# First pass of the input projection: two chunk counts and the number of warming products

## The chip, the cores and the metric

The kernel runs on one core of one Trainium2 chip. The metric is the device time of one execution in microseconds (us); the time before is the median of three runs. Beside the runs stands one execution taken with the hardware profiler, from which all views of the profile come.

## The reference

Two layers of an encoder over 256 tokens of width 2048 (batch 1, float32). Each layer makes six modulation vectors from a conditioning vector `c`, then a mixer sub-layer and a gated feed-forward sub-layer. What matters here is the beginning of the first layer:

```python
c_act = jax.nn.silu(c)
mod = c_act @ ada_w[l] + ada_b[l]
sh_a, sc_a, gt_a, sh_m, sc_m, gt_m = [t[:, None, :] for t in jnp.split(mod, 6, axis=-1)]

h = rmsnorm(x, norm_mix[l]) * (1.0 + sc_a) + sh_a
qa, ka, va, qb, kb, vb, ga, gb = split_cols(h @ w_in[l])
```

`h @ w_in` has 2048 input channels and 8704 output columns: 4608 for the queries, keys and values of two attention branches, then 2048 for each of two gates. After it come the two attentions, two projections, the gates, one output projection, and the feed-forward part.

## The kernel before

**Weights.** All big weights lie in one stream of 128x128 blocks, in the order in which TensorE uses them (`block_stream`, line 108). Sixteen blocks (1 MB) are one load. `unit_steps` (line 345) brings a load by a DMA on SyncE's queue into one of four buffers (`rawp`, line 172) and splits it into a high half (ScalarE cast, line 362) and a low half (VectorE subtraction, line 363), in two parts of eight blocks. Four buffers hold split halves (`hlp`, line 173). Every product is made of three: high x high, high x low, low x high (lines 480 to 482).

**The chunks of h.** x lies on the chip with the 2048 channels in 16 chunks of 128. One chunk of h needs two entries of the modulation: the scale and the shift of its 128 channels. Each such entry is a vector product with a 1 MB transfer (`ada`, line 243: the transfer on line 259, the product on VectorE on line 262; after a scale, line 271 makes `amod`). Then `normed` (line 570) makes the chunk: `ht` on VectorE (line 576), its high half on ScalarE (line 587), its low half on VectorE (line 588). So a chunk is three steps: two products and the chunk itself (`ada_and_h`, line 829).

**The start.** Squares of x are summed, two small matmuls (line 876) give the mean square, ScalarE adds epsilon (line 879), GpSimd takes the root (line 567), TensorE spreads it over the partitions by two transposes (line 558), ScalarE copies that to `rbs` (line 562), which each `ht` reads. Between these steps TensorE runs products that nothing reads (`warm`, line 515): `WARM_IN` (line 69) gives their number before the sums of squares, between these and the spread, and after the spread. `WARM_ROW` more follow the very first piece of work on weights (line 484).

**The passes.** In the first layer the projection for queries, keys and values goes over nine groups of 512 columns (four blocks), and over the first gate. As the chunks of h come one by one, this is done in three passes (`K_ENDS`, line 41): in the first pass group g takes chunks 0 up to its first number, and the gate's columns take chunks 0 to 5; the second pass goes on from there; the third takes the rest. `tokens` (line 468) runs one group of one pass: for each of its chunks, four blocks of the stream and six matmuls of 128x512, three for each half of the 256 tokens. At a group's end the sums are copied from PSUM by ScalarE in the first pass (line 1042, for the gate line 1078), and added by VectorE in the later ones (line 1044).

**What sets the order.** `next_block` (line 433) calls for load u + 1 when it begins load u, so one load is called ahead. At the end of each load `tick` (line 426) runs steps of `ada_and_h` until their number is on the line `FIRST_PLAN` (line 64), a table of (load, steps): 6 steps at load 0, 17 at load 10, 48 at load 42. Before a group begins, `have_h` (line 1025) runs further steps if one of its chunks has not been called yet; such steps are not counted for the line. The calls make a program in order, from which the compiler's scheduler places the instructions on each engine, with its own idea of what will be ready; each engine then runs its queue in the order so fixed, but for places that the code pins.

The table, and the pinned product that changes its number:

```python
K_ENDS = [
    [([2, 2, 2, 3, 3, 4, 4, 4, 4], 6), ([7, 7, 9, 9, 9, 10, 10, 11, 12], 13), ([KC] * 9, KC)],
...
FIRST_PLAN = [(0, 6), (10, 17), (42, 48)]
...
        warm(WARM_IN[1])
        nc.scalar.activation(out=mean_sq[:], in_=ps[:], func=AF.Identity, bias=eps[:])
```

## Time and profile before

| | us |
|---|---|
| median of three runs | 2586.0 |
| lowest and highest run | 2583.72, 2588.13 |
| profiled execution | 2584.38 |
| its span, first to last instruction | 2582.6 |
| TensorE (PE) busy | 2545.2 |
| VectorE (DVE) busy | 2209.7 |
| ScalarE (ACT) busy | 1451.2 |
| GpSimd (POOL) busy | 255.2 |

Times in the views are in us from the span's start, "mean ns" excepted. A line of the timeline gives start, duration, engine, line of the kernel, operation, what is written <- what is read, shapes and count, and in brackets the idle time before it and what ended that. A line of the waits gives who waited for whom, then the total in us, the number of times and the longest. A line of the busy time by stretches gives the stretch, its length, the busy time and number of instructions of PE, PEld (TensorE's weight loads), DVE, ACT and POOL, then the granted TensorE clock as a share of full speed, the mean busy share of the DMA engines and their GB/s. Matmul ends are modelled, so matmuls that run back to back show longer durations than the steps between their starts.

### The profile page before, as it was taken

The numbers are of one execution on the slowest core, as the hardware profiler recorded it, in microseconds if no ns is written. First come the engines' busy times: TensorE is split into PE (matmuls) and PEld (weight loads), VectorE is DVE, ScalarE is ACT, GpSimd is POOL, SyncE is SP. The second block draws the span as 40 slices with busy tenths as digits, with TensorE's granted clock in tenths as the row PEclk, the third lists the DMA queues.
The fourth block names the chain that finished last, engine by engine and source line by source line (L and its number), as shares of the span: only waits on it lengthen the run. The fifth ranks groups of instructions, "written<-read, shape, count | busy, mean of one in ns | idle before, by whom it ended". The sixth has DMA issues, their size and how long they took to land.

```text
span 2582.6 us, 41196 instructions
## 1 busy us (share of the span) xinstructions
PE 2545.2 (99%) x16204; PEld 2341.1 (91%) x16204; DVE 2209.7 (86%) x3179; ACT 1451.2 (56%) x2400; POOL 255.2 (10%) x345
## 2 busy tenths in 40 slices
PE   8999999999999999999999999999999999999999
PEld 6788888899999999999998889999999999999998
DVE  8899999898998899799987778879889987766775
ACT  5445765446653665466565666644576546654663
POOL 0000100000000000000004668730000000000000
PEclk9999999999999999999999999999999999999999
DMA  9998779886777777777767667778847775555554
GB/s 370 347 348 303 270 306 359 340 304 224 263 294 305 260 282 295 291 278 279 287 221 276 259 228 258 261 290 324 308 177 292 291 295 197 206 201 197 204 203 147
DMA packets 102149, 699.84 MB, mean 271 GB/s; under 512 B 12865, under 2 KB 15169, under 8 KB 18113
## 3 DMA queue, kind: packets, MB, share of 16 engines
q1 hardware_dynamic: 101954, 697.20, 72.8%
q8 instruction: 127, 2.08, 0.3%
q14 instruction: 68, 0.56, 0.1%
HBM read 695.06 MB, written 2.10 MB: 270 GB/s over the span
## 4 chain that ended last, share of the span: by engine, by line
PE 73%; DVE 14%; DMA 4%; issue 3%; ACT 3%; POOL 2%; SPq 0%; DVEq 0%; ACTq 0%; POOLq 0%
PE ps L405 31%; PE ps L406 15%; DVE hl L363 5%; PE ps_t L481 5%; PE ps_t L482 5%; PE ps_t L480 5%; DVE aw L262 4%; PE ps L411 3%; PE ps L409 3%; PE ps L410 3%; DMA aw<-in_aw 3%; ACT hl L362 1%; POOL p L334 1%; POOL packA L334 1%; DMA p<-in_bias 1%
## 5 line engine op out<-in xcount | busy, mean ns | idle before, releaser
L363 DVE TENSOR_TENSOR hl<-w,hl 128x1024 fp32r<-128x1024 f32 x928 | 1130.5, 1226 | 220.3 <-ACT hl L362 217.7
L362 ACT CAST hl<-w 128x1024 fp32r<-128x1024 f32 x928 | 963.3, 1046 | 590.8 <-PE ps L406 258.0
L405 PE MATMUL ps<-h,hl 128*128 128x512 f32 x2432 | 796.8, 382 | 0.0
L406 PE MATMUL ps<-h,hl 128*128 128x256 f32 x2432 | 662.9, 273 | 0.0
L405 PEld LDWEIGHTS ps<-h,hl 128*128 128x128 f32 x2432 | 459.7, 189 | 63.9
L406 PEld LDWEIGHTS ps<-h,hl 128*128 128x128 f32 x2432 | 466.9, 192 | 0.0
L262 DVE CUSTOM_DVE_ANT_0 aw<-aw,cact,ab 128x2048 f32<-128x2048 f32 x189 | 444.3, 2352 | 12.4 <-DMA aw<-in_aw 12.3
L481 PE MATMUL ps_t<-hl,h 128*128 128x512 f32 x832 | 318.5, 383 | 7.4 <-DVE hl L363 7.0
L480 PE MATMUL ps_t<-hl,h 128*128 128x512 f32 x832 | 314.9, 383 | 5.5 <-ACT hl L362 2.9
L482 PE MATMUL ps_t<-hl,h 128*128 128x512 f32 x832 | 315.9, 380 | 0.0
L481 PEld LDWEIGHTS ps_t<-hl,h 128*128 128x128 f32 x832 | 158.1, 190 | 33.8 <-DVE hl L363 12.0
L480 PEld LDWEIGHTS ps_t<-hl,h 128*128 128x128 f32 x832 | 157.3, 190 | 30.0 <-ACT hl L362 4.8
L482 PEld LDWEIGHTS ps_t<-hl,h 128*128 128x128 f32 x832 | 158.1, 190 | 22.1
L405 PE MATMUL ps<-act_o,hl 128*128 128x512 f32 x512 | 170.5, 382 | 0.0
L1189 DVE SCALAR_TENSOR_TENSOR u<-both,cw,u 128x255 f32<-128x255 f32 x304 | 146.3, 481 | 3.8
L411 PE MATMUL ps<-merged,hl 128*128 128x256 f32 x512 | 140.9, 276 | 4.4 <-DVE hl L363 4.4
L409 PE MATMUL ps<-merged,hl 128*128 128x256 f32 x512 | 140.8, 276 | 0.8 <-ACT hl L362 0.4
L410 PE MATMUL ps<-merged,hl 128*128 128x256 f32 x512 | 140.6, 275 | 0.0
L406 PE MATMUL ps<-act_o,hl 128*128 128x256 f32 x512 | 139.6, 273 | 0.0
L1211 ACT COPY both<-ps 128x256 f32<-128x256 f32 x152 | 56.2, 370 | 123.8 <-PE ps L406 122.7
L1162 DVE SCALAR_TENSOR_TENSOR x<-ps,mod,x 128x256 f32<-128x256 f32 x224 | 105.4, 482 | 21.0 <-PE ps L406 18.9
L405 PE MATMUL ps<-act_y,hl 128*128 128x512 f32 x352 | 118.3, 382 | 0.0
(267 smaller groups left out, 4656.6 us busy)
## 6 DMA issues: line engine op xcount, KB each, us to landing
w<-in_ws SPq DMA_DIRECT2D x463, 1024.0 KB, 4.9
aw<-in_aw SPq DMA_DIRECT2D x189, 1024.0 KB, 5.0
p<-in_bias SPq DMA_DIRECT2D x16, 256.0 KB, 4.6
x<-in_xT SPq DMA_DIRECT2D x4, 512.0 KB, 5.6
aw_o<-in_aw SPq DMA_DIRECT2D x2, 1024.0 KB, 12.5
out<-x SPq DMA_DIRECT2D x16, 128.0 KB, 2.4
w<-in_ws SPq DMA_DIRECT2D x2, 512.0 KB, 11.7
aw_b<-in_aw SPq DMA_DIRECT2D x1, 1024.0 KB, 17.9
```

The source lines that it names most:

```text
L262: product = nc.vector.tensor_tensor_reduce(out=raw[:], in0=raw[:], in1=cact[:], scale=1.0, scalar=ab[:, i : i + 1], op0=ALU.mult, op1=ALU. ...
L362: nc.scalar.copy(hl[:, 0], r)
L363: nc.vector.tensor_tensor(out=hl[:, 1], in0=r, in1=hl[:, 0].bitcast(F32), op=ALU.subtract)
L405: nc.tensor.matmul(ps[:], hi, act.both, start=first, stop=False)
L406: nc.tensor.matmul(ps[:, :S], lo, act.high, start=False, stop=last)
L409: nc.tensor.matmul(out, hi, act[0], start=first, stop=False)
L410: nc.tensor.matmul(ps[:, :S], hi, act[1], start=False, stop=False)
L411: nc.tensor.matmul(out, lo, act[0], start=False, stop=last)
L480: nc.tensor.matmul(ps[:], xh, hi, start=kc == kcs[0], stop=False)
L481: nc.tensor.matmul(ps[:], xh, lo, start=False, stop=False)
L482: nc.tensor.matmul(ps[:], xl, hi, start=False, stop=kc == kcs[-1])
L1189: nc.vector.scalar_tensor_tensor(out=u[:, to], in0=ps[:, of], scalar=w[:, j : j + 1], in1=u[:, to], op0=ALU.mult, op1=ALU.add)
```

## The change

In the first pass the fourth group takes two chunks of h instead of three, and the sixth three instead of four; the second pass takes up what they leave, as its own numbers stay. The stream of weights changes its order with it, since it is made from the same table. Of the products between the sums of squares and the spread of the root, four are left of twelve.

```diff
 K_ENDS = [
-    [([2, 2, 2, 3, 3, 4, 4, 4, 4], 6), ([7, 7, 9, 9, 9, 10, 10, 11, 12], 13), ([KC] * 9, KC)],
+    [([2, 2, 2, 2, 3, 3, 4, 4, 4], 6), ([7, 7, 9, 9, 9, 10, 10, 11, 12], 13), ([KC] * 9, KC)],
     [([KC] * 9, KC)],
 ]
...
-WARM_IN = [8, 12, 6]
+WARM_IN = [8, 4, 6]
```

## The prediction

> **What bounds the kernel now.** I read the page first, for the span and the engines, then the waits of TensorE (PE) by stretches, then the busy time by stretches, then the timeline of the first 120 us. The page:

> ```profile
> span 2582.6 us, 41196 instructions
> PE 2545.2 (99%) x16204; PEld 2341.1 (91%) x16204; DVE 2209.7 (86%) x3179; ACT 1451.2 (56%) x2400; POOL 255.2 (10%) x345
> ```

> PE is busy 99% of the span, so there is little to win anywhere. The change concerns the first pass, which lies in the first 120 us. Busy time of PE, PEld, DVE (VectorE), ACT (ScalarE) and POOL in four stretches, then the granted clock, the DMA share and GB/s:

> ```profile
> 24.30:60.00 35.70, 31.75 (x140) 25.60 (x139) 31.99 (x38) 21.34 (x31) 0.00 (x0) 1.00 0.96 376
> 60.00:100.00 40.00, 37.53 (x168) 31.31 (x169) 34.79 (x37) 20.90 (x29) 0.00 (x0) 1.00 0.94 355
> 100.00:120.00 20.00, 18.29 (x85) 15.72 (x84) 16.70 (x27) 8.92 (x10) 0.00 (x0) 1.00 0.88 322
> 120.00:200.00 80.00, 79.91 (x371) 69.66 (x370) 77.81 (x88) 32.91 (x36) 0.00 (x0) 1.00 0.93 351
> ```

> Up to 120 us PE, VectorE and the DMA engines are all near full, and no one of them alone is the bound; from 120 to 200 us PE has no gap. What PE waits for (total us, times, longest), from 26 to 60, 60 to 100 and 100 to 150 us:

> ```profile
> PE ps_t L480 <- ACT h L587: 1.8, 2, 1.1
> PE ps_t L480 <- ACT hl L362: 1.5, 1, 1.5
> PE ps_t L481 <- DVE hl L363: 0.2, 1, 0.2
> ```
> ```profile
> PE ps_t L481 <- DVE hl L363: 1.4, 3, 0.6
> PE ps_t L480 <- ACT hl L362: 1.4, 3, 0.6
> ```
> ```profile
> PE ps_t L481 <- DVE hl L363: 1.7, 1, 1.7
> ```

> The sum is 8.0 us: all that a better order of the first passes can bring. It is small gaps, each where a chunk of h or the halves of a weight load come late.

> **The warming products.** Eight of twelve leave the queue of PE. The timeline of the start:

> ```profile
> 13.69 2.92 PE L520 MATMUL warm<-ident 128*128 128x128 f32 x24
> ...
> 14.20 1.68 POOL L567 TENSOR_TENSOR nrs<-ms_in,mhalf 128x2 f32<-128x2 f32 x1 [12.21 <-ACT ms_in L879]
> ...
> 15.24 2.35 DVE L262 CUSTOM_DVE_ANT_0 aw<-aw,cact,ab 128x2048 f32<-128x2048 f32 x1
> ...
> 16.45 0.38 PE L558 MATMUL rb<-ident,nrs 128*128 128x128 f32 x2
> ...
> 16.86 0.37 ACT L562 COPY rbs<-rb 128x256 f32<-128x256 f32 x1 [2.74 <-PE rb L558]
> ...
> 17.63 0.16 DVE L271 SCALAR_TENSOR_TENSOR amod<-mod,nrm 128x1 f32<-128x1 f32 x1
> 17.90 0.48 DVE L576 SCALAR_TENSOR_TENSOR ht<-x,amod,rbs 128x256 f32<-128x256 f32 x1
> ```

> Twelve products are 24 matmuls in 2.92 us, 0.122 each; four end near 14.7. The root is ready at 14.20 + 1.68 = 15.9, and the spread, at 16.45 now, can start some 0.5 us earlier; rbs then ends near 16.7 instead of 17.2. But ht, the first chunk of h, also needs amod, which stands behind the second vector product (15.24 to 17.6) and itself ends at 17.8. So the 0.5 us ends in a wait that is there anyway: worth 0. The bounds are -0.5 (if VectorE took the chunk ahead of that product, which it can't, since amod needs it) and what a colder clock would cost. The cover for it is the product; with that gone 0.5 us would be gained. The clock is where this edit could do harm. PE would idle from 14.7 to 15.9 and again after the spread's own warming. The nearest rows are a longer gap later on:

> ```profile
> 276.63 0.48 PE L774 MATMUL tp<-ident,p 128*128 128x128 f32 x1 [2.55 <-ACT p L763]
> ```
> ```profile
> 270.00:280.00 10.00, 7.45 (x30) 6.07 (x30) 8.74 (x18) 6.05 (x18) 0.00 (x0) 0.83 0.84 297
> ```

> A gap of 2.55 us is followed by a mean clock of 0.83 over 10 us, which is 0.17 x 10 / 0.5 = 3.4 us at half speed, a loss of at most 1.7 us; the 1.7 us gap of the third wait list left the clock at 1.00 (row 100 to 120). An idle of 1.2 us is nearer to the second. I take 0; even half speed there would be largely hidden, since sixteen warming products (L484) stand between the first piece and the next weights.

> [...]

> **The two moved pieces.** Call one chunk of h through one group of four blocks a piece: six matmuls. 34 steps lie between these two rows:

> ```profile
> 107.73 0.38 PE L481 MATMUL ps_t<-hl,h 128*128 128x512 f32 x1
> ...
> 115.07 0.38 PE L482 MATMUL ps_t<-hl,h 128*128 128x512 f32 x1
> ```

> so one matmul is 7.34 / 34 = 0.216 us, a piece 1.30, a load (16 blocks, 1 MB) four pieces or 5.18. Two pieces leave the first pass and stand in the second: PE work, loads, copies (L1042) and adds (L1044) are the same in number, so this is 0 by itself. What moves is the need and the calls. Counting pieces from 0, chunk 2 of h is needed in piece 10 instead of 8, chunk 3 in 17 instead of 15; chunk 4 in 30 instead of 32 and chunk 5 in 31 instead of 33, because the gates begin two pieces sooner. Of the calls (a: a product of L262 with its transfer; h: a chunk; w: a load) the old order is a4 a5 w2 h2 a6 w3 a7 h3 w4 a8 w5 a9 w6 h4 w7 a10 a11 h5 w8 a12 w9 a13 w10 h6; the new one a4 a5 w2 h2 w3 a6 w4 a7 h3 a8 w5 a9 w6 h4 w7 a10 a11 h5 a12 w8 a13 w9 h6 w10. On SyncE w3 passes a6, w4 passes a7, and from w8 to w15 one more step is ahead; with the ninth chunk of h, which the old code calls out of turn at piece 62, both are level again by load 16.

> Chunks 2 and 3, VectorE, ACT and PE:

> ```profile
> 31.60 2.35 DVE L262 CUSTOM_DVE_ANT_0 aw<-aw,cact,ab 128x2048 f32<-128x2048 f32 x1
> ...
> 34.18 0.48 DVE L576 SCALAR_TENSOR_TENSOR ht<-x,amod,rbs 128x256 f32<-128x256 f32 x1
> ...
> 35.12 1.98 ACT L362 CAST hl<-w 128x1024 fp32r<-128x1024 f32 x2
> ...
> 36.18 2.36 DVE L363 TENSOR_TENSOR hl<-w,hl 128x1024 fp32r<-128x1024 f32 x2 [0.45 <-ACT hl L362]
> 36.20 1.13 PE L480 MATMUL ps_t<-hl,h 128*128 128x512 f32 x4 [1.53 <-ACT hl L362]
> ...
> 38.46 2.35 DVE L262 CUSTOM_DVE_ANT_0 aw<-aw,cact,ab 128x2048 f32<-128x2048 f32 x1
> ```
> ```profile
> 40.73 2.36 DVE L363 TENSOR_TENSOR hl<-w,hl 128x1024 fp32r<-128x1024 f32 x2
> ...
> 46.66 0.48 PE L480 MATMUL ps_t<-hl,h 128*128 128x512 f32 x1 [0.74 <-ACT h L587]
> ```

> At 36.20 PE waits 1.53 us for the cast of w2, not for chunk 2: VectorE and ACT ran chunk 2 first, though w2 was called first. A chunk holds them 36.18 - 34.18 = 2.0 us, a product 40.73 - 38.46 = 2.27. Piece 8 still needs w2, and nothing in the change puts w2 ahead of chunk 2: the gap stays (between -1.5 and 0; 0 by the order of this row). Chunk 3 (0.74) is needed 2.6 us later, but a7 now gets the buffer that w2 frees at 38.5, not the one that a5 frees at 33.95 (31.60 + 2.35), and w3 and w4 stand before it: supply slips by as much as the need. Between -0.74 and +1.5; 0.

> Chunk 5 and w8:

> ```profile
> 70.96 2.36 DVE L363 TENSOR_TENSOR hl<-w,hl 128x1024 fp32r<-128x1024 f32 x2 [0.45 <-ACT hl L362]
> 73.24 2.35 DVE L262 CUSTOM_DVE_ANT_0 aw<-aw,cact,ab 128x2048 f32<-128x2048 f32 x1
> ```
> ```profile
> 70.98 0.70 PE L480 MATMUL ps_t<-hl,h 128*128 128x512 f32 x2 [0.52 <-ACT hl L362]
> 71.93 0.70 PE L480 MATMUL ps_t<-hl,h 128*128 128x512 f32 x2 [0.25 <-ACT hl L362]
> ```

> PE comes to w8 as it is made. VectorE is free at 70.96 - 0.45 = 70.5; with a12 ahead, the low halves start near 70.5 + 2.3 = 72.8 and the first (half of 2.36) is there at 74.0. PE has high products until about 72.3, so it stands 1.7 us. Chunk 6 ahead of w9 costs VectorE 2.0 us more, of which I let PE see 1.6. From w10 on that is repaid: in the old order chunk 6 ran ahead of w10, in the new one it lies behind already, and the stalls of the second wait list that follow w8 fall away. Of 3.3 us I leave 1.1 at load 10 (an estimate between 0 and 3.3, from the 2.0 of a chunk that is no longer ahead). This lag lasts to load 16:

> ```profile
> 112.25 0.69 DVE L1044 TENSOR_TENSOR packA<-ps_t,packA 128x512 f32<-128x512 f32 x1 [1.76 <-PE ps_t L482]
> ...
> 116.31 2.35 DVE L363 TENSOR_TENSOR hl<-w,hl 128x1024 fp32r<-128x1024 f32 x2
> ```
> ```profile
> 117.58 0.48 PE L481 MATMUL ps_t<-hl,h 128*128 128x512 f32 x1 [1.71 <-DVE hl L363]
> ```

> VectorE stands 1.76 us for the sums of the second pass's second group, then adds, then runs a product and a chunk, and only then w16; PE pays 1.71. In the new order this group ends two pieces (2.6 us) sooner against w16, so the wait and PE's 1.71 go. Sum: 0 + 0 + 0 + 1.1 - 1.7 = -0.6 us. Underneath lies that by load 16 the same products, chunks, loads and bytes have passed in both: only idle can be won. The profiled execution took 2584.4 us (span 2582.6), so 2583.8; the median of the runs stands 1.6 above it, and I forecast 2585.4.

> **Rivals.** *Faster:* with chunk 2 called half a load later, w2 comes first on ACT and VectorE, chunk 3 is in time, the stall at w16 goes and no lag takes their place: -1.5 - 0.7 - 1.7 = -3.9 against the median of 2586.0, 2582.1; if all 8.0 us go, 2578.0. For it: chunk 2's call now stands after the pieces of load 1. Against it: w2 was called ahead before, and lost its place all the same. *Slower:* a12 and chunk 6 ahead of w8 and w9 cost 1.7 + 1.6, not repaid since VectorE has no spare time in its 31.99 of 35.7 us, and the two idles bring one stretch at half speed, 1.7: +5.0, 2591.0. It decides at idle times near 2 us within one such stretch. For it: 2.55 us was enough at 276. Against it: 1.71 was not. *No change in fact:* the order in which the instructions are placed on each engine is not the order of the calls (chunk 2 before w2 shows it), so both orders may come out nearly alike: 2586.0.

> **How the numbers follow.** Forecast 0.55, faster 0.20, slower 0.12, no change 0.13. The forecast's unknowns (-1.5, -0.74 to +1.5, lag 0 to 3.3) make 2582 to 2589; the rivals widen the range to 2580.5 to 2590.5. 0.2%, about what a measurement here can tell, is 5.2 us: below 2580.8 lies only the outer part of the faster case, and a little for gaps later in the trace that happen to move: 0.13. Above 2591.2 lies about half of the slower case and such chance: 0.10. Within: 0.77.

> **What would show it.** Right: in the changed profile the transposes of L558 start near 16.0 and ht still at 17.9; a gap near 36 us; gaps of 1 to 2 us at 71 to 80; none at 117; from 120 us on the same trace within a microsecond. Wrong: the gap at 36 gone (faster), a granted clock below 1.00 before 120 us (slower), or gaps beyond 200 us that came or went, which this working does not see.

## The result and the profile after

| | before | after |
|---|---|---|
| median (14 runs each) | 2583.4 us | 2587.6 us |
| lowest and highest run | 2580.4, 2588.13 | 2585.04, 2592.28 |
| ratio, 95% interval | | 1.0020 (1.0013 to 1.0026) |
| profiled execution, its span | 2584.38, 2582.6 | 2589.55, 2587.7 |

The change made the kernel slower by 4.2 us, or 0.2%. The median before is now 2583.4 us, from 14 runs, where the first three gave 2586.0. The page of the changed kernel:

```profile
span 2587.7 us, 41164 instructions
PE 2545.8 (98%) x16188; PEld 2340.2 (90%) x16188; DVE 2209.5 (85%) x3179; ACT 1453.8 (56%) x2400; POOL 260.3 (10%) x345
```

PE has the same busy time in a span that is 5.1 us longer. Busy time by the same stretches as before the change, and three short ones:

```profile
24.30:60.00 35.70, 31.36 (x134) 25.33 (x133) 29.39 (x33) 19.82 (x29) 0.00 (x0) 0.95 0.89 349
60.00:100.00 40.00, 35.59 (x152) 29.00 (x151) 34.75 (x41) 21.05 (x28) 0.00 (x0) 0.96 0.93 368
100.00:120.00 20.00, 18.10 (x83) 15.52 (x82) 15.77 (x27) 8.73 (x10) 0.00 (x0) 0.99 0.78 282
120.00:200.00 80.00, 80.00 (x365) 69.79 (x365) 74.27 (x84) 33.33 (x35) 0.00 (x0) 0.98 0.89 333
37.50:40.90 3.40, 3.27 (x8) 2.62 (x9) 3.40 (x4) 1.97 (x3) 0.00 (x0) 0.50 0.59 198
78.40:81.80 3.40, 3.26 (x8) 2.60 (x9) 3.40 (x3) 2.25 (x3) 0.00 (x0) 0.51 0.77 292
119.40:122.80 3.40, 3.40 (x10) 2.68 (x9) 3.40 (x5) 0.73 (x2) 0.00 (x0) 0.50 0.56 186
```

The column before the DMA share is the granted clock. It was 1.00 in all four stretches of before; now it falls below, and the short rows show where: three times about 3.4 us at half speed. In such a stretch PE counts as busy, so its busy share hides half of the loss. What PE waited for from 26 to 150 us (8.0 us before):

```profile
PE ps_t L480 <- ACT hl L362: 4.5, 5, 2.0
PE ps_t L481 <- DVE hl L363: 2.5, 2, 1.9
PE ps_t L482 <- DVE h L588: 2.0, 2, 1.0
PE ps_t L480 <- ACT h L587: 1.7, 3, 0.7
```

10.7 us, so 2.7 us more of idle. Set side by side, the starts of the pieces (us; piece p is the p-th set of six matmuls as PE ran them) show where PE fell behind:

```
piece       8      12     16     24     32     36     40     56      64      68      80
before    36.20  41.88  48.06  59.00  70.98  76.78  83.27  104.92  115.28  122.44  138.33
after     36.68  44.08  49.26  62.58  77.28  85.01  90.19  110.91  125.12  130.30  145.84
behind     0.48   2.20   1.20   3.58   6.30   8.23   6.93    5.99    9.84    7.87    7.52
```

Three places: pieces 8 to 24, 24 to 36 and 60 to 68. The 2.7 us of idle and three stretches at half speed, each worth at most 3.4 x 0.5 = 1.7 us, make up to 7.8 us, an estimate; 7.5 were measured at piece 80. At the end of the span 5.1 us are left: 1.0 came back between 535 and 680 us, 1.2 after 1675 us. These stretches differ from run to run too, and their gaps were not followed up.

**The first place.** ScalarE at piece 8, and what VectorE and ScalarE did for chunk 3:

```profile
34.06 1.23 ACT L1042 COPY packB<-ps_t 128x512 f32<-128x512 f32 x2 [1.35 <-PE ps_t L482]
35.19 0.51 ACT L587 ACTIVATE h<-ht,mod 128x256 fp32r<-128x256 f32 x1
35.60 3.87 ACT L362 CAST hl<-w 128x1024 fp32r<-128x1024 f32 x4
...
53.16 0.51 ACT L587 ACTIVATE h<-ht,mod 128x256 fp32r<-128x256 f32 x1 [3.98 <-DVE ht L576]
```
```profile
47.79 2.36 DVE L363 TENSOR_TENSOR hl<-w,hl 128x1024 fp32r<-128x1024 f32 x2 [4.22 <-ACT hl L362]
50.06 2.35 DVE L262 CUSTOM_DVE_ANT_0 aw<-aw,cact,ab 128x2048 f32<-128x2048 f32 x1
```

The fourth group now ends on piece 7, the last of its load. Its copy waits for PE, and behind it in ScalarE's queue stand chunk 2 and the cast that PE waits for. Later VectorE idles 4.22 us for the casts of load 4, with the product of chunk 3 queued behind; the high half of chunk 3 comes at 53.16. The product's transfer had landed near 43.8 us, so the product did not wait for it. In the kernel before the high half came at 46.10:

```profile
46.10 0.51 ACT L587 ACTIVATE h<-ht,mod 128x256 fp32r<-128x256 f32 x1 [3.44 <-DVE ht L576]
```

About half of the 3.6 us at piece 24 is half speed: in a second profiled execution of the same kernel (`after_again`, below) none followed the gap at piece 8, and PE was 1.9 us behind at piece 24.

**The second place.** SyncE's queue before and after, then PE, ScalarE and VectorE at piece 32:

```profile
61.37 0.33 SPq L351 DMA_DIRECT2D w<-in_ws  x1
64.22 0.33 SPq L259 DMA_DIRECT2D aw<-in_aw  x1
```
```profile
58.09 7.18 SPq L259 DMA_DIRECT2D aw<-in_aw  x3
67.22 0.33 SPq L351 DMA_DIRECT2D w<-in_ws  x1
```
```profile
75.18 0.70 PE L482 MATMUL ps_t<-hl,h 128*128 128x512 f32 x2 [1.00 <-DVE h L588]
77.28 0.70 PE L480 MATMUL ps_t<-hl,h 128*128 128x512 f32 x2 [1.40 <-ACT hl L362]
78.54 0.79 PE L481 MATMUL ps_t<-hl,h 128*128 128x512 f32 x1 [0.56 <-DVE hl L363]
...
80.41 0.63 PE L480 MATMUL ps_t<-hl,h 128*128 128x512 f32 x1
80.84 0.63 PE L481 MATMUL ps_t<-hl,h 128*128 128x512 f32 x1
```
```profile
75.70 0.59 ACT L1078 COPY ya<-ps_t 128x512 f32<-128x512 f32 x1 [2.70 <-PE ps_t L482]
76.18 1.99 ACT L362 CAST hl<-w 128x1024 fp32r<-128x1024 f32 x2
```
```profile
72.37 2.35 DVE L262 CUSTOM_DVE_ANT_0 aw<-aw,cact,ab 128x2048 f32<-128x2048 f32 x1
...
74.64 0.48 DVE L588 SCALAR_TENSOR_TENSOR h<-ht,mod,h 128x256 fp32r<-128x256 f32 x1
```

The transfer of load 8 starts at 67.22 instead of 61.37: a12 has passed it, and PE was 3.6 us late already. It landed near 72.4 us, but its cast came only at 76.18, behind the copy of the gate's first group, which ends on piece 31, again the last of a load. That copy waited for PE, and PE had waited 1.00 us for the low half of chunk 5, which stood behind the product of a12 on VectorE. The last two rows of PE are 0.43 us apart where 0.216 is the step at full speed.

**The third place.** VectorE and PE at piece 60:

```profile
115.65 0.69 DVE L1044 TENSOR_TENSOR packA<-ps_t,packA 128x512 f32<-128x512 f32 x1 [2.87 <-PE ps_t L482]
...
117.31 2.35 DVE L363 TENSOR_TENSOR hl<-w,hl 128x1024 fp32r<-128x1024 f32 x2
```
```profile
118.58 0.48 PE L481 MATMUL ps_t<-hl,h 128*128 128x512 f32 x1 [1.90 <-DVE hl L363]
```

The second group of the second pass ends on piece 59, the last of load 14. VectorE waits for its sums 2.87 us, adds, and only then makes the low halves of load 15, which PE needs at once.

### The profile page after: what moved, and what is told of

Its sections match the earlier page's. It is cut to its first block, busy times and chain, and to the rows that moved or that the text cites. A ratio compares the mean times of both kernels' runs of the same rounds, so it can differ in the third digit from the quotient of the medians.

```text
span 2587.7 us, 41164 instructions
## 1 busy us (share of the span) xinstructions
PE 2545.8 (98%) x16188; PEld 2340.2 (90%) x16188; DVE 2209.5 (85%) x3179; ACT 1453.8 (56%) x2400; POOL 260.3 (10%) x345
## 3 DMA queue, kind: packets, MB, share of 16 engines
q1 hardware_dynamic: 101954, 697.20, 72.3%
## 4 chain that ended last, share of the span: by engine, by line
PE 77%; DVE 12%; issue 3%; POOL 3%; ACT 3%; DMA 2%; SPq 0%; DVEq 0%; ACTq 0%; POOLq 0%
PE ps L405 31%; PE ps L406 15%; PE ps_t L482 5%; PE ps_t L481 5%; PE ps_t L480 5%; PE ps L411 4%; DVE hl L363 4%; PE ps L409 4%; PE ps L410 4%; DVE aw L262 3%; DMA aw<-in_aw 2%; ACT hl L362 1%; POOL p L334 1%; POOL packA L334 1%; PE sc L743 1%
## 5 line engine op out<-in xcount | busy, mean ns | idle before, releaser
L363 DVE TENSOR_TENSOR hl<-w,hl 128x1024 fp32r<-128x1024 f32 x928 | 1130.0, 1225 | 224.5 <-ACT hl L362 222.7
L362 ACT CAST hl<-w 128x1024 fp32r<-128x1024 f32 x928 | 965.0, 1047 | 596.8 <-PE ps L406 264.8
L262 DVE CUSTOM_DVE_ANT_0 aw<-aw,cact,ab 128x2048 f32<-128x2048 f32 x189 | 443.8, 2349 | 10.5 <-DMA aw<-in_aw 10.4
L481 PE MATMUL ps_t<-hl,h 128*128 128x512 f32 x832 | 319.3, 384 | 6.5 <-DVE hl L363 6.4
L480 PE MATMUL ps_t<-hl,h 128*128 128x512 f32 x832 | 318.2, 385 | 7.5 <-ACT hl L362 4.5
L482 PE MATMUL ps_t<-hl,h 128*128 128x512 f32 x832 | 318.0, 383 | 2.0 <-DVE h L588 2.0
L480 PEld LDWEIGHTS ps_t<-hl,h 128*128 128x128 f32 x832 | 158.4, 191 | 32.9 <-ACT hl L362 6.5
L481 PEld LDWEIGHTS ps_t<-hl,h 128*128 128x128 f32 x832 | 159.2, 191 | 31.8 <-DVE hl L363 9.5
L482 PEld LDWEIGHTS ps_t<-hl,h 128*128 128x128 f32 x832 | 158.7, 191 | 25.5 <-DVE h L588 3.0
L567 POOL TENSOR_TENSOR nrs<-nss,mhalf 128x2 f32<-128x2 f32 x3 | 2.1, 697 | 1172.4 <-DVE nss L638 1172.4
```

What stands on the lines that cost most here:

```text
L262: product = nc.vector.tensor_tensor_reduce(out=raw[:], in0=raw[:], in1=cact[:], scale=1.0, scalar=ab[:, i : i + 1], op0=ALU.mult, op1=ALU. ...
L362: nc.scalar.copy(hl[:, 0], r)
L363: nc.vector.tensor_tensor(out=hl[:, 1], in0=r, in1=hl[:, 0].bitcast(F32), op=ALU.subtract)
L480: nc.tensor.matmul(ps[:], xh, hi, start=kc == kcs[0], stop=False)
L481: nc.tensor.matmul(ps[:], xh, lo, start=False, stop=False)
L482: nc.tensor.matmul(ps[:], xl, hi, start=False, stop=kc == kcs[-1])
```

## The experiments

Theory 1: loads that pass products, and products that pass loads, make the gaps. Theory 2: groups that end on the last piece of a load put their copies and adds ahead of the next load's halves. Beside both, half speed after the gaps, and the rival that the warming products did it. All ratios are against the kernel before on the same chip.

**The two edits apart.** `k_only` has `WARM_IN = [8, 12, 6]` with the new table:

> The table of chunk counts alone, with twelve warming products as before. If the table makes the loss (it changes the order of casts, copies, products and loads on ScalarE, VectorE and SyncE, and so PE's gaps in the first 120 us, and these gaps bring half speed), this run shows all of it: +4 us against the kernel before (3 to 6), with gaps near 2 us at 35, 76 and 117 us. If the warming products make it, 0 (-1.5 to +1.5).

2589.96 (five runs) against 2582.35 us, ratio 1.0033 (1.0020 to 1.0045). The gaps are 2.0, 1.4 and 1.9 us as in the changed kernel. `warm_only` is the reverse:

```diff
-WARM_IN = [8, 12, 6]
+WARM_IN = [8, 4, 6]
```

> The old table with four warming products. If the table makes the loss: 0 (-1 to +1), ht still at 17.9 us and the first product on weights still at 19.0. If the warming products make it, by an idle PE in the first 16 us and a colder clock after it: +4 us.

2580.75 against 2582.35 us, 0.9991 (0.9982 to 1.0000). The table makes the whole loss; the fewer warming products cost no time, at the edge of a gain. In this profiled execution half speed did come at 20.54 us: PE was 0.8 us behind at piece 4, and 0.25 ahead at piece 8.

**Filling the gaps.** `fill_after` adds warming products to the changed kernel, keyed by the number of pieces done:

```diff
+FILL = {1: 16, 8: 8, 32: 6, 64: 8}
...
-                if self.l == 0 and self.u == 1 and self.at == 4:
-                    warm(WARM_ROW)
+                if self.l == 0 and self.at % 4 == 0:
+                    warm(FILL.get(4 * self.u - 4 + self.at // 4, 0))
```

> The changed kernel with 8, 6 and 8 more warming products ahead of pieces 8, 32 and 64, where PE stands idle for 2.0, 1.4 and 1.9 us. If the loss is to a large part half speed after these idles (three stretches of 3.4 us at half speed, up to 1.7 us each), granted clock 1.00 up to 125 us and -3 to -5 us against the changed kernel, so -1 to +1.5 against the one before. If the loss is the idle itself or the later order, the clock rises and the time stays within 1 us of the changed kernel, +3.5 to +5 against the one before.

2586.61 against 2582.35 us, 1.0018 (1.0009 to 1.0026): the expected gain is not there, and by the expectation this speaks for the idle itself. But the trial was badly placed: the third gap lies in piece 60, so the products ahead of piece 64 cost their own time there, and one half-speed stretch remained at 74 us. It was mended:

```diff
-FILL = {1: 16, 8: 8, 32: 6, 64: 8}
+FILL = {1: 16, 8: 8, 31: 4, 32: 6, 60: 6}
```

> The changed kernel with 8, 4, 6 and 6 more warming products ahead of pieces 8, 31, 32 and 60, now at the very pieces where PE stands (the earlier trial had its last ones ahead of piece 64, behind the gap, where they cost PE their own 1.9 us). The order of all other instructions is that of the changed kernel. If half speed after the idles is most of the loss: granted clock 1.00 from 30 to 125 us, PE 2 to 3 us behind the kernel before at 130 us instead of 7.5, and 3 to 5 us less than the changed kernel on the same chip, -1 to +1.5 us against the kernel before. If the idles themselves are the loss: PE 5 us or more behind at 130 us, within 1.5 us of the changed kernel.

Beside it on the same chip ran the changed kernel as it is:

> The changed kernel as it is, on the same chip as the trial with warming products, so that the two stand side by side: +4 us (3 to 6) against the kernel before, with half speed after the gaps near 36, 77 and 118 us in most executions.

`after_again`: 2588.48 against 2583.69 us, 1.0021 (1.0012 to 1.0030). `fill_after2`: 2585.72 us, 1.0010 (1.0000 to 1.0019). The first three stretches of `after_again`, then of `fill_after2`:

```profile
24.30:60.00 35.70, 31.34 (x141) 25.49 (x139) 30.34 (x37) 20.50 (x31) 0.00 (x0) 1.00 0.91 367
60.00:100.00 40.00, 36.32 (x151) 29.25 (x150) 34.78 (x37) 21.07 (x27) 0.00 (x0) 0.91 0.95 352
100.00:120.00 20.00, 18.10 (x80) 15.40 (x79) 16.20 (x27) 8.09 (x10) 0.00 (x0) 0.95 0.78 284
```
```profile
24.30:60.00 35.70, 33.13 (x157) 27.55 (x156) 30.40 (x36) 20.36 (x31) 0.00 (x0) 1.00 0.92 367
60.00:100.00 40.00, 37.55 (x180) 31.73 (x179) 35.92 (x39) 21.67 (x29) 0.00 (x0) 1.00 0.95 361
100.00:120.00 20.00, 19.44 (x96) 16.89 (x95) 16.63 (x27) 8.68 (x10) 0.00 (x0) 1.00 0.79 304
```

With the same order of all other work the clock stays at 1.00, and at piece 80 PE is 2.65 us behind the kernel before instead of 6.06 (`after_again`). So 2588.48 - 2585.72 = 2.8 us of the 4.8 by which `after_again` is slower go with half speed; the other 2.0 are left to idle and to what the products themselves cost. That is a little under the 3 to 5 that was expected, and the scatter of the runs leaves it open by nearly 2 us either way. The mean granted clock over the runs agrees: 0.9984 before, 0.9964 changed, 0.9975 filled.

**Theory 1.** `k_plan` holds back the extra step:

```diff
-FIRST_PLAN = [(0, 6), (10, 17), (42, 48)]
+FIRST_PLAN = [(0, 6), (6, 13), (7, 13), (10, 16), (42, 47)]
```

> The changed kernel with the line of steps lowered by one from load 7 on, so that the vector product of step 19 is called after load 8 and not before it, and as many steps are called by each later load as in the kernel before. If the extra step makes the gaps between 72 and 78 us (0.6, 1.0, 1.4, 0.6) and the half speed after them, these fall to below 1 us in sum and the time falls by 3 to 4 us, to 0 to +1.5 against the kernel before. If the copies of sums that stand ahead of the casts on ScalarE make them, the gaps stay and the time is within 1 us of the changed kernel.

2585.44 against 2582.35 us, 1.0013 (1.0004 to 1.0022). The gaps between 70 and 78 us shrink to 0.6 and 0.2, and from piece 24 to 32 PE loses nothing (1.91 to 1.80 us behind). ScalarE now runs the cast of load 8 ahead of the copy:

```profile
71.24 1.98 ACT L362 CAST hl<-w 128x1024 fp32r<-128x1024 f32 x2
73.12 1.06 ACT L1078 COPY ya<-ps_t 128x512 f32<-128x512 f32 x2
```

The extra step made the second place. The time is a miss even so, +3.1 us where 0 to +1.5 was expected: the gap in piece 60 stays, with 1.5 us, and between pieces 68 and 72 PE loses 1.8 us that the changed kernel did not lose. `k_calls` also calls a6 and a7 early again:

```diff
+FIRST_PLAN = [(0, 6), (1, 8), (2, 10), (6, 14), (7, 14), (10, 17), (42, 48)]
```

> The changed kernel with the line of steps bent so that each product and chunk is called against the loads as in the kernel before: a6 before w3, a7 before w4, and no extra step from load 7 to load 15. Theory 1, that the loss comes from loads that pass products and products that pass loads: VectorE's idle of 4.2 us near 45 and the gaps at 53 to 55 and 72 to 78 us fall to what the kernel before has, PE is less than 1.5 us behind it at 130 us, time 0 to +1.5 us against it. Theory 2, that the ends of the groups, now on other pieces, put copies of sums ahead of the casts on ScalarE: the gaps stay, PE is 4 us or more behind at 130 us, time +3 to +5 us.

2585.47 against 2583.11 us, 1.0015 (1.0006 to 1.0024), PE 5.2 us behind at piece 80: a miss for theory 1, though the time lies between the two theories. With the calls as before the gap at piece 8 stays at 2.0 us with half speed after it, and from piece 60 on PE loses 1.9 us more. At piece 24 it is 4.7 us behind, not less than the 3.6 of the changed kernel, so loads that pass products don't by themselves explain the first place. `k_calls_fill` fills the gap at piece 8:

```diff
+FILL = {1: 16, 8: 7}
```

> The kernel of the bent line with seven more warming products ahead of piece 8, in the 2 us gap near 35 us, which the bent line leaves. If half speed after that gap is a part of the loss: no half speed before 100 us, and about 1 us less than with the bent line alone, -1 to +0.5 us against the kernel before. If not: the same as with the bent line alone within 0.5 us.

2585.95 us, 1.0008 (0.9999 to 1.0017): no half speed from 25 to 275 us, but a stretch at 20.61 us, so that PE was 0.9 us behind at piece 4 already. As a time it is inconclusive, since the two intervals overlap and the medians stand the other way.

**Each group alone.**

```diff
-    [([2, 2, 2, 3, 3, 4, 4, 4, 4], 6), ...
+    [([2, 2, 2, 2, 3, 4, 4, 4, 4], 6), ...   (g3_only)
+    [([2, 2, 2, 3, 3, 3, 4, 4, 4], 6), ...   (g5_only)
```

> The old table with the fourth group alone cut from three chunks to two, twelve warming products. Theory 1: the load w3 passes the product a6 as in the changed kernel, so the gap near 35 us stays at 2.0 us and VectorE's idle near 45 us is there: +2 to +4 us against the kernel before. Theory 2: the copies of the fourth group come ahead of the cast of load 2, +2 to +4 as well; but the gate's groups then end on pieces 33, 39, 45 and 51, never on the last piece of a load, so that there is no gap of over 1 us at 76 us.

> The old table with the sixth group alone cut from four chunks to three, twelve warming products. Up to piece 12 it is the kernel before, so the gap near 35 us is 1.5 us. Theory 1: the extra step ahead from load 7 on remains, with gaps near 72 to 78 us of 2 us or more in sum and half speed after them in many executions: +1.5 to +3 us. Theory 2: the group ends lie on no load's last piece from the sixth group on, so 0 to +1 us.

`g3_only` 2581.03 us, 0.9992 (0.9983 to 1.0001); `g5_only` 2582.99 us, 1.0002 (0.9993 to 1.0011), both against 2583.11. Theory 1 expected a loss from each and falls here as a full account. `g3_only` has the gap of 2.0 us at piece 8, half speed after it and 4.3 us of lag at piece 24, and still ends level: at piece 64 both kernels are 1.8 us behind, at piece 68 they are 0.2 ahead. Cutting one group turns all later ends by one piece: the gate's first group ends on piece 32, the second pass's second group on piece 60, each the first of a load, and the 1.71 us that the kernel before pays at load 16 are gone. Cutting two turns them by two, onto pieces 31 and 59, the last of a load. (The gate's groups end on pieces 32, 38, 44 and 50 in `g3_only` too, not on those that its expectation names.) But `g5_only` has the gaps that theory 1 named, 0.8 and 1.5 us at piece 32 with half speed after them and 4.0 us of lag at piece 36. No group ends on the last piece of a load just ahead of them, so theory 2 has no place for them.

**Theory 2.** `after_g1` moves one such end, that of the second pass's second group, by one piece (the ends behind it in this pass move along):

```diff
-... ([7, 7, 9, 9, 9, 10, 10, 11, 12], 13), ...
+... ([7, 8, 9, 9, 9, 10, 10, 11, 12], 13), ...
```

> The changed kernel whose second pass gives its second group eight chunks instead of seven (the third pass takes one less), so that this group ends on piece 60, the first of load 15, and no longer on piece 59, the last of load 14. Theory 2, that a group which ends on the last piece of a load puts its adds and copies ahead of the next load's halves, and PE then stands: the gap of 1.9 us near 117 us and the half speed after it go, PE loses 0 to 0.5 us between pieces 56 and 68 instead of 1.9 (the kernel before pays its 1.7 there), time 2 to 3.5 us under the changed kernel, +1 to +2 us against the one before. Theory 1, that only the passed loads and the extra step count: within 1 us of the changed kernel.

2585.94 against 2583.20 us, 1.0010 (1.0002 to 1.0019). VectorE now:

```profile
114.76 2.36 DVE L363 TENSOR_TENSOR hl<-w,hl 128x1024 fp32r<-128x1024 f32 x2 [0.45 <-ACT hl L362]
117.34 1.29 DVE L1044 TENSOR_TENSOR packA<-ps_t,packA 128x512 f32<-128x512 f32 x2 [0.22 <-PE ps_t L482]
```

The low halves of load 15 come before the add; the lag is 5.74 us at pieces 56 and 64 alike and 3.77 at 68. So the end makes the third place. In time it shows less clearly: 1.0010 stands beside the 1.0021 of `after_again`, on another chip and with intervals that overlap. But theory 2 isn't all either: with `k_plan` the gate's group still ends on piece 31 and the gap of 1.4 us is gone. In the kernel before groups end on pieces 11, 15, 19, 23, 27, 39 and 51, the last of their loads; behind 23 and 39 PE waits 0.6 and 1.1 us, behind the others at most 0.2. The reading that fits these runs is that an end on a load's last piece costs where the next load's halves haven't been made ahead of it; a passed transfer or product makes them late, and the end then adds its wait. For the first place this is argued from the rows alone: no run moved the end on piece 7 by itself. `k_plan_g1` has this and the line of `k_plan`:

> The same second group of eight chunks, with the line of steps lowered by one from load 7 on. Theory 2 with theory 1 for the gaps of 72 to 78 us: both places of loss are gone, PE at 130 us is within 1 us of the kernel before or ahead of it, time -1 to +1 us. If one place is not understood, PE is 2 us or more behind and the time +1.5 us or more.

2582.11 us, 0.9993 (0.9984 to 1.0002): level with the kernel before. PE's waits from 26 to 150 us:

```profile
PE ps_t L480 <- ACT hl L362: 3.1, 4, 2.0
PE ps_t L481 <- DVE hl L363: 2.2, 3, 1.5
PE ps_t L480 <- ACT h L587: 1.7, 3, 0.7
PE ps_t L482 <- DVE h L588: 1.0, 1, 1.0
```

8.0 us, as in the kernel before. PE is still 1.8 us behind at piece 80, more than the 1 us that was expected, with one stretch at half speed behind it, at 38.03 us; in this execution 1.5 us of that came back between 247 and 291 us, and that stretch was not followed up. One more comparison lies in this run: up to piece 56 its code is that of `k_plan`, but in its profiled execution half speed followed the gap at piece 8, in that of `k_plan` it did not. At piece 48 they are 2.31 and 0.45 us behind: one half-speed stretch there cost 1.9 us, and VectorE did not hide it.

**A better kernel.** The fourth group's cut and the four warming products together, then with `FILL = {1: 16, 8: 7}` too:

> The fourth group alone cut to two chunks, with four warming products instead of twelve. Each of the two alone came out about 2 us under the kernel before. If they add up, -2 to -4 us; the group's cut turns the second pass by one piece, so that PE does not stand at load 16. If the gains were chance, 0.

> The same with seven more warming products ahead of piece 8, in the gap of 2.0 us at 35 us that the cut leaves. If half speed after that gap is a cost, another -0.5 to -1.5 us, -3 to -5 us against the kernel before, with a granted clock of 1.00 from 30 to 45 us. If VectorE sets the time in that stretch, so that half speed is hidden, the same as without.

2580.47 us, 0.9992 (0.9984 to 1.0001), and 2581.02 us, 0.9990 (0.9981 to 0.9998), against 2583.20. That is 2.7 and 2.2 us less, at the low end of the -2 to -4 us that was hoped for, and less than the 2.1 and 1.6 us of the two alone together; only the second ratio excludes no change, and just so. The added products showed no gain, and in the profiled execution without them no half speed followed the gap at piece 8 that they were to cover. Against `g3_only`, where it did follow, PE of `g3_warm` is 0.7 instead of 2.1 us behind at piece 12, and 3.4 us in both at piece 16: there the stretch was hidden after all.

## Why the prediction was wrong

The forecast was 0.6 us less, the result 4.2 us more. The time of 2587.6 us lies in the range, but that range was laid around a before of 2586.0 us, and the kernel moved the other way. Three steps of the sum failed: the term at load 16, put at -1.7 us, where PE fell 1.9 us further behind; the lag at load 10, put at 1.1 us and measured at 6.9; and half speed, put at nothing, which came three times.

- **The warming products:** right in time. The spread starts at 15.94, ht still at 17.90, and `warm_only` lost nothing. The clock was not quite safe, as the prediction took it to be: of the twelve profiled executions with four products, four have a stretch at half speed that begins between 16.0 and 20.6 us, of the four with twelve products none.

```profile
15.94 0.43 PE L558 MATMUL rb<-ident,nrs 128*128 128x128 f32 x2 [0.95 <-POOL nrs L567]
```
```profile
17.90 0.48 DVE L576 SCALAR_TENSOR_TENSOR ht<-x,amod,rbs 128x256 f32<-128x256 f32 x1
```

- **Chunk 2:** the gap stays, as put, but at 2.0 instead of 1.5 us, and with half speed behind it.
- **Chunk 3:** "supply slips by as much as the need" was wrong. The need slips by 2.6 us, the chunk by 53.16 - 46.10 = 7.1, and PE is 3.6 us behind at piece 24 (1.9 without half speed, in `after_again`). I had counted the transfer's buffer and not the casts of load 4 that stand ahead of the product.
- **The lag at load 10:** put at 1.1 us, measured 6.9 (of which 3.6 stood at piece 24). That a12 ahead of w8 costs PE was right; the price was not. PE waited 1.00 us for chunk 5 behind a12, 1.40 us for the cast of w8, which fell behind a copy that waits for PE, and 0.56 us for the low half, and half speed followed. Chunk 6 ahead of w9, put at 1.6 us, left no gap: PE has none between 78.6 and 116 us.
- **Load 16:** "-1.7" failed. The group does end two pieces sooner against w16, but that puts its end on the last piece of load 14, and load 15 pays instead: it saves the 1.71 us and pays 1.90 us of idle and a stretch at half speed, and from piece 56 to 68 the lag grew by 1.9 us. One piece sooner, as in `g3_only`, gives the gain that I had counted.
- **The clock:** I kept half speed to the slow rival, with one stretch, and took 1.7 us of idle as harmless. It came three times in this execution; `fill_after2` shows 2.8 us for it. The slow rival came nearest: a12 ahead of w8, not repaid, and idle that brings half speed. That its +5.0 us stands so close to the measured 4.2 is in part luck: its 1.6 us for chunk 6 did not appear, and it lacked the first place, the ends of groups and two of the three stretches at half speed.
- **"By load 16 the same work has passed in both, so only idle can be won":** true, and it says nothing of idle that can be lost. VectorE's busy time from 24.3 to 60 us fell from 31.99 to 29.39 us of 35.7.

## What to carry to other kernels

Where sums are copied or added on the engines that also prepare the next weights, write down on which piece of a load each group ends, and whether the next load is ready by then: if it isn't, an end on the last piece makes the preparation wait for the sums and PE for the preparation (2.87 us on VectorE and 1.90 us on PE at piece 60 of the changed kernel). Here one cut, which turns all later ends by one piece, was level, and two such cuts lost 0.2%. And price an idle gap of PE near 2 us at up to twice its length, for the half speed that may follow it: an estimate from the gap of 2.0 us at piece 8, which a stretch of 3.4 us at half speed followed, worth at most 1.7 us, in six of nine profiled executions. Products that nothing reads, placed in the gap at piece 8, kept the clock at full speed after it in all four profiled executions that had them (1.00 from 24.3 to 60 us in `fill_after2`); with others at the later gaps they saved 2.8 us in one comparison, and alone nothing that could be told in two more.
